# Letting the planner of a hybrid RWKV-7 / DeltaNet layer count TensorE's instructions, with ranks set anew

## The chip, the cores and the metric

One core of one Trainium2 chip runs the whole layer in one launch. The metric is device time in microseconds (us), lower is better. Three runs of the kernel before took 2218.86, 2225.49 and 2235.87 us; the median is 2225.49.

## What is computed

One diffusion-backbone layer in fp32: 256 latent tokens and 256 context tokens, width 2048. The reference, cut to its stages:

```python
h  = modulate(rmsnorm(x, norm1_w), sh1, sc1)       # sh, sc, gt from silu(c) @ w_ada
hc = modulate(rmsnorm(ctx, norm1_w), csh1, csc1)
rw, cv, z, ab, gt = split(h @ w_in)                # the same for hc
o_a = rwkv_readout(bidirectional RWKV-7 scan of 16 heads x 64)     # context state starts the latents
o_b = gdn_readout(bidirectional chunked DeltaNet of 8 heads x 128) # triangular solve per chunk of 64
y = (sigmoid(g_a) * (o_a @ p_a) + sigmoid(g_b) * (o_b @ p_b)) @ w_out
x = x + gt1 * y
x = x + gt2 * swiglu(modulate(rmsnorm(x, norm2_w), sh2, sc2), w_gate_up, w_down)
return rmsnorm(x, final_norm_w)
```

## The kernel before

**Stages.** A first stage (to about 136 us) makes the modulation and the low-rank columns. Then comes the *weave* (about 136 to 1290 us): the input projection, the RWKV mixer in 8 pairs of heads and the DeltaNet mixer in 8 heads, interleaved. Behind it stand the products with `p_a`, `p_b`, `w_out` and the feed-forward part. Every large product is done in three fp32r matmuls, high by high, high by low and low by high; the weights are split into `whi` (a cast on ScalarE) and `wlo` (a subtraction on VectorE) after their load into `wraw`.

**Main products.** In the weave the generator `products()` makes the projection: a product is 16 k-steps of three matmuls `mm<-hxh,whi`, `mm<-hxl,whi`, `mm<-hxh,wlo`, 512 columns wide where context is needed and 256 wide otherwise. They need only weights and the input, so they serve as fill for TensorE. The 40 gate columns (`GATES_A`, `GATES_B`) are spread over pairs and heads by hand.

**Chains.** For each pair or head other generators carry the chain: `prepare`, `grams` (lists of 32 small matmuls, 64x64, into `pa`), `inverse` (`invert()`: two lists of 64 matmuls `pi<-arena` and `pi<-arena,Tx` with 32x16 outputs, then two of 32 with 32x32, with VectorE work between them), `scan`, `values`, and for heads `head_grams`, `head_inverse`, `head_scan`, `features`, `decays`, `tokens`. `lowrank` makes the matmuls `s<-lin,wraw`. `ada_rest` accumulates further modulation columns.

**What sets the order.** All five engines run their instructions in the order in which the weave hands them out. `Weave.run` is a greedy planner at build time: each generator holds one operation or one list of TensorE operations; for each it estimates the earliest start (engine free, last result plus `HOP`), and the smallest (start, rank) goes next. A list is cut to `LAT['grp']` = 32 operations for TensorE at a time; costs come from `Lane`. Ranks (`RANK`, plus 10 per pair or head) break ties, the lowest first; main products have rank 900. Outside the weave a scheduler of the framework sets the order.

**Lines.** In the profile every operation that the weave emits has line L147, the `return op` call of `Lane`. L370 and L371 are the split of the weights behind the weave, L380 to L382 the matmuls of `gemm`.

**Instruction size.** An fp32r matmul or a transpose becomes two of TensorE's instructions (a weight load and a matmul), a plain fp32 matmul four (two passes of each). So the 64 small fp32 matmuls of one `pi` list are 256 instructions. TensorE's instructions, 48234 with its semaphore waits, are fetched from memory while the kernel runs, by a DMA queue of kind "instruction".

Of the kernel before, what the change touches and what calls it, by code (L numbers as in the profile page):

```python
# [12 lines left out]
F32R = mybir.dt.float32r  # L13
# [11 lines left out]
NPAIR = 8  # L25
NGH = 8
DECAY = 0.6065306597126334
GATES_A, GATES_B = (6, 2, 3, 3, 0, 1, 4, 3), (2, 2, 0, 1, 0, 2, 10, 1)

RANK = dict(cast=-94, lowrank=60, prepare=59, grams=34, inverse=-56, values=6, scan=-39, begin=196, head_scan=145, head_inverse=100, head_grams=123, decays=137, tokens=77, features=120, gate_out=137, lowrank_out=105, row_tile=486)  # L30
LAT = dict(dma=2.04, hop=0.255, own=0.092, grp=32, cg=4, turn=0.17)
LNEXP = "natural_log_exp_and_others"
SIGM = "sigmoid_and_others"
UNIT = 64 * 64 + 64
# [65 lines left out]
        return t.rearrange(f"p ({' '.join(ax)}) -> p {' '.join(ax)}", **dict(zip(ax, shape[1:])))  # L100


HOP = LAT['hop']


# [7 lines left out]
class Lane:  # L113
# [5 lines left out]
    def __getattr__(self, name):  # L119

        def op(out, *a, **k):
            if name == "preload_act_table_set":
                return Op(self, 1.3, lambda: self.engine.preload_act_table_set(out))
            if name == "dma_start":
                return Op(self, 0.6 if self.each > 0.0012 else 0.33, lambda: self.engine.dma_start(out, *a))
            n = int(np.prod(out.shape[1:]))
            kind = "full"
            if name == "transpose" and len(a) == 2:
                cost = 0.109
            elif name == "matmul":  # L130
                rows, m = a[0].shape[0], out.shape[0]
                if a[0].dtype == F32R:
                    cost, kind = 0.0035 + 0.000448 * n, "split"
                elif rows <= 64 and m <= 64:
                    cost, kind = (0.01 + 0.00037 * n if rows < 64 else 0.01 + 0.00075 * n), (rows, m)
                elif m <= 64:
                    cost, kind = 0.058 if m == 64 else 0.14, (rows, m)
                else:
                    cost = (0.0054 + 0.00167 * n) * (1.22 if rows == 96 else 1)
            else:  # L140
                psum = a and getattr(a[0], "tensor", None) is not None and "PSum" in type(a[0].tensor).__name__
                cost = (self.psum if psum else self.fixed) + self.each * n
                if name == "tensor_tensor_scan":
                    cost *= 1.9
                elif name == "scalar_tensor_tensor" and not psum:
                    cost *= 1.2
            return Op(self, cost, lambda: getattr(self.engine, name)(out, *a, **k), kind)  # L147
        return op
# [33 lines left out]
        return self.pool.tile([P, 512], F32, tag=self.tag, name=self.tag)  # L182


class Weave:


# [2 lines left out]

    def __init__(self):
        self.work, self.free, self.done, self.now, self.kind = [], {}, {}, 0.0, "split"

    def add(self, rank, gen, at=None):
        now = self.now
# [45 lines left out]
    def run(self):  # L241
        while self.work:
            for w in list(self.work):
                if w[5] is not None and not isinstance(w[5], (list, float)) and self.there(w):
                    self.step(w, self.take(w))
            best = None
            for w in self.work:
                if isinstance(w[5], float):
                    key = (w[3], w[0])
                    if best is None or key < best[0]:  # L250
                        best = (key, w, None)
                elif isinstance(w[5], list):
                    lane = w[5][0].lane
                    at = w[3] + (0.0 if w[4] is None else lane.own if w[4] is lane else HOP)
                    key = (max(self.free.get(lane, 0.0), at), w[0])
                    if best is None or key < best[0]:
                        best = (key, w, lane)
            if best is None:
                if any(w[5] is not None and not isinstance(w[5], (list, float)) and self.there(w) for w in self.work):
                    continue  # L260
                assert not self.work, [w[5] for w in self.work]
                return
            (start, _), w, lane = best
            if lane is None:
                w[5] = None
                assert w[3] < 1e5, [x[5] for x in self.work]
                self.step(w, None)
                continue
            ops, rest, w[4] = w[5], None, lane
            if lane is self.tensor:  # L270
                ops, rest = ops[:LAT['grp']], ops[LAT['grp']:]
                if ops[0].kind != self.kind:
                    start += LAT["turn"] if isinstance(ops[0].kind, tuple) or isinstance(self.kind, tuple) else 0.02
                self.kind = ops[-1].kind
            w[5] = rest or None
            got = [o.call() for o in ops]
            w[3] = self.free[lane] = start + sum(o.cost for o in ops)
            if rest:
                w[4] = None
            else:  # L280
                self.step(w, got[-1])


def emit(ctx: ExitStack, tc, A, out, dbg=None):
    nc = tc.nc
    V, S, G, Q = nc.vector, nc.scalar, nc.gpsimd, nc.sync
    E = nc.tensor
    global weave
    weave = Weave()
    dq = Loads(Q)  # L290
# [131 lines left out]
    with tc.tile_pool(name="p0", bufs=1) as p0, \  # L422
# [100 lines left out]
        for part in range(NE + 1):  # L523
            if part < NE:
                ps = pst(pmm, "mm")
            for c in range(2):
# [6 lines left out]
                if c == 0 and part < NE:  # L533
                    w = low_split(part)
# [212 lines left out]
    def lowrank():  # L747
# [17 lines left out]
        for p in range(NPAIR):  # L765
# [12 lines left out]
            for j in (0, 2, 1, 3):  # L778
                ps = yield psb
                yield e.matmul(ps, w[:96, 4 * (p % 2) + j], lin[:, j], start=True, stop=True)  # L780
                weave.add(RANK['lowrank_out'], lowrank_out(p, j, ps, out[j]))

    def prepare(p):
# [75 lines left out]
        if p + 1 < NPAIR:  # L859
            weave.add(10 * p + 10 + RANK['prepare'], prepare(p + 1))  # L860

# [220 lines left out]
    def products():  # L1082
# [24 lines left out]
        while todo or nxt:  # L1107
            if nxt is None:
# [4 lines left out]
                if nxt[0] == "g":  # L1113
                    nxt = "g", next(gate_next)
                weave.add(RANK['cast'], cast(source(*nxt), i))
            what, p = nxt
# [3 lines left out]
            for k in range(KT):  # L1120
                if k == 4:
                    nxt = choose()
                    if nxt is not None:
                        if nxt[0] == "g":
                            nxt = "g", next(gate_next)
                        weave.add(RANK['cast'], cast(source(*nxt), i + 1))
                if k % LAT['cg'] == 0:
# [7 lines left out]
            if what == "g":  # L1135
                weave.add(RANK['gate_out'], gate_out(rs, p, ps))
            else:
# [9 lines left out]
    first = {"laR": [P, 2, 4, 2, 64], "KB": [P, 2, 8, 64], "VX0": [P, 8, 2, 64], "VX1": [P, 8, 2, 64], "KBx": [P, 2, 8, 2, 64],  # L1147
             "ivx": [P, 16, 64], "Y": [P, 4, 64], "bon": [P, T], "y2": [P, T], "y3": [P, T]}

    class Shared:  # L1150


        def __init__(self):
            self.arena = Places(None, arena, *gplaces)
            self.inX = [None, None]
# [475 lines left out]
    for j in range(KT):  # L1631
# [13 lines left out]
        elif j % 3 == 2 and j < 12:  # L1645
            hi, lo = (W4[:, i, j // 3] for i in range(2))
            for c in range(2):
                k, raw = slice(8 * c, 8 * c + 8), coming.pop(0)
# [3 lines left out]
    r = rms_scale(x1p, [ssum, sq], T, "rs")  # L1652
# [6 lines left out]
    with tc.tile_pool(name="fp", bufs=1, reuse_waits="tile") as fp:  # L1659
# [19 lines left out]
        for j in range(NH):  # L1679
# [12 lines left out]
            if 2 <= j < 34:  # L1692

                for a in range(2):
                    c = (j - 2) // 2
                    i = 2 * (j % 2) + a
                    w = fp.tile([P, 512], F32, tag="aw", name="aw", bufs=3)
# [19 lines left out]
        r = rms_scale(x1p, [ssum, sq], T, "rs", keep=True)  # L1717
# [99 lines left out]
```

## Time and profile before

| | |
|---|---|
| median of 3 runs | 2225.49 us (2218.86 to 2235.87) |
| the profiled execution | 2228.24 us, span 2226.1 us |
| TensorE (PE) busy | 2117.7 us, 95% |
| VectorE (DVE) busy | 1571.3 us, 71% |
| ScalarE (ACT) busy | 1068.5 us, 48% |
| mean granted TensorE clock | 0.982 |

The span runs from the first to the last instruction; the execution's own time is 2.1 us more. Busy PE time is modelled from start times, so a row's duration overlaps the next row; start to start is the better measure of what a matmul costs. In the timeline, `[1.74 <-issue]` behind a row says that the engine was idle 1.74 us before it and waited for no semaphore that the profile shows. The granted clock of a stretch is a share of full speed.

### The profile page before, as it was taken

To read this page: it belongs to the slowest core of one execution; us is meant where nothing else is said; L and a number is where in the kernel's file an instruction comes from. 1 tells how busy PE (TensorE), PEld (TensorE's weight loads), DVE (VectorE), ACT (ScalarE), POOL (GpSimd) and SP (SyncE) were. 2 spreads that over 40 slices of the span, in tenths; PEclk is the share of its full clock that TensorE was granted. 3 is DMA by queue.
4 is the path that set the end of the run, shared out by engine and by line. 5 is a ranking of instruction groups with operands and counts; after the bars stand their busy time and mean duration, and the time that the engine had idled before them with its cause. 6 is when DMAs were issued, how large, how long until landed. Compare 5 with 4: busy or idle time off the path is not lost.

```text
span 2226.1 us, 56729 instructions
## 1 busy us (share of the span) xinstructions
PE 2117.7 (95%) x23996; PEld 1913.4 (86%) x23996; DVE 1571.3 (71%) x3197; ACT 1068.5 (48%) x1853; POOL 120.4 (5%) x203
## 2 busy tenths in 40 slices
PE   6998899899999999999999989999999999999998
PEld 3875678778888778878788889999999999999997
DVE  3456778787988778999998778855666665444454
ACT  3258745544454455445554455534444444444443
POOL 0000100100000011011110010100000000000000
PEclk9999899999999999999999999999999999999999
DMA  9966444444444445566567797937777776566665
GB/s 385 413 181 180 133 121 112 111 114 115 118 119 139 112 146 164 175 180 184 172 201 239 257 339 257 348 100 225 235 235 235 236 236 203 190 186 186 190 190 160
DMA packets 234494, 435.29 MB, mean 196 GB/s; under 512 B 115328, under 2 KB 129664, under 8 KB 229888
## 3 DMA queue, kind: packets, MB, share of 16 engines
q1 hardware_dynamic: 206304, 355.11, 50.8%
q0 software_dynamic: 14112, 51.39, 7.2%
q10 hardware_dynamic: 13824, 25.17, 3.4%
q8 instruction: 188, 3.08, 0.6%
q14 instruction: 66, 0.54, 0.1%
HBM read 405.76 MB, written 25.84 MB: 194 GB/s over the span
## 4 chain that ended last, share of the span: by engine, by line
issue 45%; PE 29%; DVE 12%; DMA 9%; ACT 3%; POOL 1%; SPq 1%; POOLq 0%; DVEq 0%; ACTq 0%
PE mm L147 14%; PE pa L147 5%; DVE arena L147 4%; DVE wlo L147 2%; PE s L147 2%; PE pi L147 2%; PE mm L382 1%; PE mm L381 1%; PE mm L380 1%; DMA aw<-ada_rest 1%; DMA aw<-ada_first 1%; DVE aw L147 1%; ACT arena L147 1%; PE mm L475 1%; DMA wr<-wgu 1%
## 5 line engine op out<-in xcount | busy, mean ns | idle before, releaser
L371 DVE TENSOR_TENSOR wlo<-wraw,whi 128x1024 fp32r<-128x1024 f32 x328 | 392.7, 1198 | 318.7 <-ACT whi L370 316.0
L370 ACT CAST whi<-wraw 128x1024 fp32r<-128x1024 f32 x328 | 336.9, 1028 | 463.3 <-PE mm L381 409.2
L147 PE MATMUL mm<-hxh,wlo 128*128 128x256 f32 (+1 forms) x1376 | 465.3, 338 | 10.0 <-DVE wlo L147 9.2
L147 PE MATMUL mm<-hxh,whi 128*128 128x256 f32 (+1 forms) x1376 | 463.8, 337 | 2.0 <-DVE arena L147 1.2
L147 PE MATMUL mm<-hxl,whi 128*128 128x256 f32 (+1 forms) x1376 | 461.1, 335 | 0.0
L382 PE MATMUL mm<-hfh,wlo 128*128 128x256 f32 x1344 | 375.1, 279 | 0.4 <-DVE wlo L371 0.4
L380 PE MATMUL mm<-hfh,whi 128*128 128x256 f32 x1344 | 375.0, 279 | 0.0
L381 PE MATMUL mm<-hfl,whi 128*128 128x256 f32 x1344 | 374.9, 279 | 0.0
L147 PEld LDWEIGHTS mm<-hxh,wlo 128*128 128x128 f32 x1376 | 263.1, 191 | 39.6 <-DVE wlo L147 14.4
L147 PEld LDWEIGHTS mm<-hxh,whi 128*128 128x128 f32 x1376 | 263.3, 191 | 25.6 <-issue 5.6
L147 PEld LDWEIGHTS mm<-hxl,whi 128*128 128x128 f32 x1376 | 263.4, 191 | 23.6 <-issue 3.9
L147 DVE TENSOR_TENSOR wlo<-wraw,whi 128x512 fp32r<-128x512 f32 x344 | 239.9, 698 | 34.9 <-ACT whi L147 33.5
L147 ACT CAST whi<-wraw 128x512 fp32r<-128x512 f32 x344 | 204.5, 616 | 110.6 <-PE mm L147 84.4
L382 PEld LDWEIGHTS mm<-hfh,wlo 128*128 128x128 f32 x1344 | 252.8, 188 | 0.7 <-DVE wlo L371 0.6
L380 PEld LDWEIGHTS mm<-hfh,whi 128*128 128x128 f32 x1344 | 252.9, 188 | 0.0
L381 PEld LDWEIGHTS mm<-hfl,whi 128*128 128x128 f32 x1344 | 252.8, 188 | 0.0
L147 DVE TENSOR_TENSOR arena<-arena 128x28 f32<-128x28 f32 (+12 forms) x538 | 139.0, 261 | 23.5 <-DMA arena<-scr 9.2
L380 PE MATMUL mm<-za,whi 128*128 128x256 f32 x512 | 142.9, 279 | 0.0
L382 PE MATMUL mm<-za,wlo 128*128 128x256 f32 x512 | 142.7, 279 | 0.0
L381 PE MATMUL mm<-za,whi 128*128 128x256 f32 x512 | 142.7, 279 | 0.0
L147 ACT ACTIVATE arena<-arena 128x512 f32<-128x512 f32 (+2 forms) x132 | 76.4, 593 | 76.4 <-DVE arena L147 59.5
L380 PEld LDWEIGHTS mm<-za,whi 128*128 128x128 f32 x512 | 96.3, 188 | 0.0
(332 smaller groups left out, 3943.6 us busy)
## 6 DMA issues: line engine op xcount, KB each, us to landing
wraw<-w SPq DMA_DIRECT2D x172, 512.0 KB, 4.0
wraw<-wgu SPq DMA_DIRECT2D x168, 512.0 KB, 4.6
aw<-ada_rest POOLq DMA_DIRECT2D x96, 512.0 KB, 5.2
aw<-ada_first SPq DMA_DIRECT2D x32, 1024.0 KB, 13.2
wraw<-wdn SPq DMA_DIRECT2D x64, 448.0 KB, 3.6
wraw<-wout SPq DMA_DIRECT2D x32, 512.0 KB, 6.9
aw<-ada_gt ACTq DMA_DIRECT2D x64, 256.0 KB, 4.8
wraw<-wdn SPq DMA_DIRECT2D x32, 512.0 KB, 3.7
```

What stands on the lines that cost most here:

```text
L147: return Op(self, cost, lambda: getattr(self.engine, name)(out, *a, **k), kind)
L370: S.copy(hi[:, c, :M], raw[:, c, :M])
L371: V.tensor_sub(lo[:, c, :M], raw[:, c, :M], hi[:, c, :M].bitcast(F32))
L380: E.matmul(ps, hi, Xh[:, k, :n], start=first and i == 0, stop=False)
L381: E.matmul(ps, hi, Xl[:, k, :n], start=False, stop=False)
L382: E.matmul(ps, lo, Xh[:, k, :n], start=False, stop=last and i == len(wt) - 1)
L475: E.matmul(ps[32 * g:32 * g + 32, 0:P], ckr[:, k].rearrange("p a b -> p (a b)"), aws[e, c][:, i, g], start=k == 0, stop=k == KT - 1)
```

## The change

The planner gets a count of TensorE's instructions. A wrapper `Words` around the engine counts two or four for each matmul or transpose emitted, from the start of the program. `Weave.late` walks through a list and asks at each block boundary (every 256 instructions, the first at 193) whether the block would be there: it was asked for 40 instructions before the previous boundary, or when the block before arrived, and comes 4.2 us later. What is missing is added to the list's estimated start, so another generator, most often `products()`, may go first. Operations keep their costs; transposes become a kind of their own ("turn"), which adds the small cost of 0.02 us at a change of kind to the plan. At the same time `RANK`, the hop and the gates per pair and head are set to other numbers; the sums of the gates stay 22 and 18. With the wrapper every matmul has line L198.

```diff
-GATES_A, GATES_B = (6, 2, 3, 3, 0, 1, 4, 3), (2, 2, 0, 1, 0, 2, 10, 1)
+GATES_A, GATES_B = (6, 3, 2, 3, 0, 1, 4, 3), (3, 2, 0, 1, 1, 1, 9, 1)
-RANK = dict(cast=-94, lowrank=60, ... inverse=-56, values=6, scan=-39, ... head_grams=123, decays=137, tokens=77, ...
+RANK = dict(cast=-98, lowrank=164, ... inverse=-70, values=-6, scan=-95, ... head_grams=132, decays=132, tokens=73, ...
+BLOCK = dict(size=256, first=193, ahead=40, time=4.2, base=8, waits=1.0072)
+class Words:
+        def op(out, a, *r, **k):
+            self.n += (2 if name == "transpose" or a.dtype == F32R else 4) * BLOCK["waits"]
+            return getattr(self.engine, name)(out, a, *r, **k)
...
+    def late(self, ops, start):
+        n, t, b, here, asked, late = self.tensor.engine.n, start, self.block, self.here, self.asked, 0.0
+        if b is None:
+            b = int(n - BLOCK["first"]) // BLOCK["size"] + 1
+        for o in ops:
+            edge = BLOCK["first"] + BLOCK["size"] * b
+            if asked is None and n >= edge - BLOCK["ahead"]:
+                asked = max(t, here)
+            if n >= edge:
+                if t < here:
+                    late += here - t
+                    t = here
+                b, here, asked = b + 1, (t if asked is None else asked) + BLOCK["time"], None
+            n += self.words(o) * BLOCK["waits"]
+            t += o.cost
+        return late, (b, here, asked)
...
-                    at = w[3] + (0.0 if w[4] is None else lane.own if w[4] is lane else HOP)
-                    key = (max(self.free.get(lane, 0.0), at), w[0])
+                    at = max(self.free.get(lane, 0.0), w[3] + (0.0 if w[4] is None else lane.own if w[4] is lane else HOP))
+                    if lane is self.tensor and (best is None or at <= best[0][0]):
+                        at += self.late(w[5][:LAT["grp"]], at)[0]
+                    key = (at, w[0])
```

What it moves is seen in TensorE's rows. **The first pair's inverse.** Before, the list of 64 in `inverse(0)` is followed at once by the `grams` list of the second pair (rows of two, which go on below):

```order
L147 MATMUL s<-lin,wraw 128x512
L147 MATMUL mm<-hxh,wlo 128x512
L147 MATMUL pi<-arena 32x16 x64
L147 MATMUL pa<-kh,arena 64x64 x2
L147 MATMUL pa<-arena,kh 64x64 x2
```

Now that `grams` list stands ahead, a low-rank matmul lies between the two, and main products follow the list:

```order
L198 MATMUL pa<-kh,arena 64x64 x2
L198 MATMUL pa<-arena,kh 64x64 x2
L198 MATMUL s<-lin,wraw 128x512
L198 MATMUL pi<-arena 32x16 x64
L198 MATMUL s<-lin,wraw 128x512
L198 MATMUL mm<-hxl,whi 128x512
```

The rows show that the 256 instructions of `pi` no longer have another small list right behind them; the `grams` list itself now follows main and low-rank matmuls.

**The second pair's inverse.** Before, its two lists of 64 stood with one list of 16 (the readout of the first pair's scan) between them:

```order
L147 MATMUL mm<-hxh,wlo 128x512
L147 MATMUL pi<-arena 32x16 x64
L147 MATMUL s<-laR,VX 64x64 x16
L147 MATMUL pi<-arena,Tx 32x16 x64
L147 MATMUL pa<-sgd,g_3568 128x256
L147 MATMUL pa<-C,arena 128x128 x2
```

Now that readout stands ahead of both, and wide work lies between the two lists:

```order
L198 MATMUL s<-laR,VX 64x64 x16
L198 MATMUL pi<-arena 32x16 x64
L198 MATMUL pa<-sgd,g_3573 128x256
L198 MATMUL pa<-C,arena 128x128 x2
L198 MATMUL mm<-hxl,whi 128x512
L198 MATMUL mm<-hxh,wlo 128x512
L198 MATMUL mm<-hxh,whi 128x512
L198 MATMUL pa<-Y,C 128x256
...
L198 MATMUL pa<-C,arena 128x128 x2
L198 MATMUL pi<-arena,Tx 32x16 x64
L198 MATMUL pa<-y_3639,C 128x256
```

Seven main matmuls, two 256-wide fp32 matmuls and four transposes have come between the lists of 64.

**The end of the weave.** Before, the last main products stood behind the last head's inverse, among the first matmuls of its `head_scan` (`s<-TF,keg`):

```order
L147 MATMUL s<-TF_10841,keg 128x128 x3
L147 MATMUL pa<-C,arow 128x128 x2
L147 MATMUL mm<-hxh,whi 128x256
L147 MATMUL mm<-hxl,whi 128x256
...
L147 MATMUL s<-TF_10841,keg 128x128 x3
L147 MATMUL s<-inX,TF_10841 128x128 x2
L380 MATMUL mm<-oah,whi 128x256 x2
```

Now they end inside that inverse, and the products with `p_a` (`mm<-oah,whi` and its kin) fill from there on:

```order
L198 MATMUL pi<-inX,qo 32x32 x16
L198 MATMUL mm<-hxh,wlo 128x256
L198 MATMUL mm<-oah,whi 128x256 x2
L198 MATMUL pi<-qo,inX 32x32 x16
L198 MATMUL mm<-oal,whi 128x256
```

The last head's readout (`s<-arena,C`) stood behind 122 of the 384 matmuls with `p_a`, and now stands behind 242.

More of the change, by code (lines that the diff above doesn't have):

```diff
@@ L27 @@
 DECAY = 0.6065306597126334
-GATES_A, GATES_B = (6, 2, 3, 3, 0, 1, 4, 3), (2, 2, 0, 1, 0, 2, 10, 1)
-RANK = dict(cast=-94, lowrank=60, prepare=59, grams=34, inverse=-56, values=6, scan=-39, begin=196, head_scan=145, head_inverse=100, head_grams=123, decays=137, tokens=77, features=120, gate_out=137, lowrank_out=105, row_tile=486)
-LAT = dict(dma=2.04, hop=0.255, own=0.092, grp=32, cg=4, turn=0.17)
+GATES_A, GATES_B = (6, 3, 2, 3, 0, 1, 4, 3), (3, 2, 0, 1, 1, 1, 9, 1)
+RANK = dict(cast=-98, lowrank=164, prepare=59, grams=34, inverse=-70, values=-6, scan=-95, begin=196, head_scan=145, head_inverse=100, head_grams=132, decays=132, tokens=73, features=120, gate_out=137, lowrank_out=105, row_tile=496)
+LAT = dict(dma=2.04, hop=0.2729, own=0.092, grp=32, cg=4, turn=0.17)
 LNEXP = "natural_log_exp_and_others"
@@ L128, in op @@
             if name == "transpose" and len(a) == 2:
-                cost = 0.109
+                cost, kind = 0.109, "turn"
             elif name == "matmul":
@@ L182, in tile, with __init__, __getattr__ @@
         return self.pool.tile([P, 512], F32, tag=self.tag, name=self.tag)
+class Words:
+    def __init__(self, engine):
+        self.engine, self.n = engine, BLOCK["base"]
+    def __getattr__(self, name):
+        if name not in ("matmul", "transpose"):
+            return getattr(self.engine, name)
+        def op(out, a, *r, **k):
+            self.n += (2 if name == "transpose" or a.dtype == F32R else 4) * BLOCK["waits"]
+            return getattr(self.engine, name)(out, a, *r, **k)
+        return op
 class Weave:
@@ L192, in __init__, with words @@
         self.work, self.free, self.done, self.now, self.kind = [], {}, {}, 0.0, "split"
+        self.block, self.here, self.asked = None, 0.0, None
+    def words(self, op):
+        return 2 if op.kind in ("split", "turn") else 4
+    def late(self, ops, start):
[14 more added lines that the diff above has]
+        return late, (b, here, asked)
     def add(self, rank, gen, at=None):
@@ L274, in run @@
                 self.kind = ops[-1].kind
+                self.block, self.here, self.asked = self.late(ops, start)[1]
             w[5] = rest or None
@@ L286, in emit @@
     V, S, G, Q = nc.vector, nc.scalar, nc.gpsimd, nc.sync
-    E = nc.tensor
+    E = Words(nc.tensor)
     global weave
```

## Prediction

> **What bounds the kernel now.** I read the page first, then TensorE's waits, then the timeline around the longest stops, then the granted clock.
>
> ```profile
> span 2226.1 us, 56729 instructions
> PE 2117.7 (95%) x23996; PEld 1913.4 (86%) x23996; DVE 1571.3 (71%) x3197; ACT 1068.5 (48%) x1853; POOL 120.4 (5%) x203
> q8 instruction: 188, 3.08, 0.6%
> ```
>
> TensorE is the bound, so a gain must come from its idle time or from a slow clock. The third row (queue, packets, MB, share) matters here: 188 packets bring 3.08 MB, 16 KB each; over TensorE's 48234 instructions that is one packet for 256. TensorE's waits, in total, times, longest:
>
> ```profile
> PE pi L147 <- issue: 11.8, 8, 2.2
> PE mm L147 <- DVE wlo L147: 9.2, 13, 2.0
> PE s L147 <- DVE Vn L147: 6.2, 7, 2.1
> PE pa L147 <- issue: 4.1, 3, 1.8
> ```
>
> The first and last row are 11 stops of **15.9 us** in which TensorE waited for nothing that the profile shows. The middle rows are ordinary waits for VectorE. Where the 11 lie, the timeline shows:
>
> ```profile
> 242.32 0.23 PE L147 MATMUL pa<-arena,kh 64*64 64x64 f32 x2
> 244.28 0.37 PE L147 MATMUL pa<-kh,arena 64*64 64x64 f32 x2 [1.74 <-issue]
> ...
> 317.36 0.31 PE L147 MATMUL pi<-arena 32*32 32x16 f32 x14 [0.48 <-issue]
> 321.63 0.57 PE L147 MATMUL pi<-arena,Tx 32*32 32x16 f32 x46 [2.08 <-issue]
> 416.80 1.88 PE L147 MATMUL pi<-arena,Tx 32*32 32x16 f32 x123 [1.22 <-issue]
> 420.92 0.81 PE L147 MATMUL pa<-laR,arena 64*64 64x64 f32 x20 [1.82 <-issue]
> ```
>
> A stop falls in the middle of a list that needs no new data. Counted along TensorE's rows, all 11 stand at instruction 193 plus a multiple of 256, within two. Consecutive stops end 321.63 - 317.36 = 4.27 and 420.92 - 416.80 = 4.12 us apart. I read this as: a block of 256 instructions comes no faster than one in some 4.2 us. How fast a list eats a block:
>
> ```profile
> L147 PE MATMUL pi<-arena,Tx 32*32 32x16 f32 x1024 | 12.6, 188 | 10.0 <-issue 9.4 <-DVE arena L147 0.6
> L147 PE MATMUL pa<-KB,X 64*64 64x64 f32 x1024 | 19.1, 221 | 0.0
> ```
>
> A pass of the first kind costs 12.6/1024 = 0.012 us, so 64 matmuls (128 passes, one whole block) take 1.6 us; the second kind's 0.019 us makes 2.4 us. Two such lists in a row must stop.
>
> [...]
>
> A second cost follows the stops. These stretches, found by the clock's steps, begin with or soon after a stop and run at half clock (columns: length, busy PE, PEld, DVE, ACT, POOL, granted clock, DMA):
>
> ```profile
> 244.32:254.56 10.24, 10.24 (x180) 6.89 (x180) 7.51 (x16) 5.01 (x11) 0.00 (x0) 0.50 0.48 157
> 322.83:326.24 3.41, 3.41 (x10) 2.74 (x11) 2.06 (x7) 2.96 (x10) 0.00 (x0) 0.50 0.06 17
> 414.99:425.23 10.24, 6.89 (x175) 6.45 (x176) 6.82 (x16) 1.03 (x4) 0.00 (x0) 0.50 0.41 111
> 486.67:490.08 3.41, 3.41 (x52) 3.27 (x44) 3.13 (x10) 1.63 (x5) 0.00 (x0) 0.50 0.22 59
> 548.11:551.52 3.41, 3.41 (x18) 3.04 (x18) 2.65 (x7) 1.30 (x5) 0.00 (x0) 0.50 0.02 5
> 626.61:630.03 3.42, 3.42 (x19) 3.42 (x18) 3.35 (x7) 1.58 (x6) 0.00 (x0) 0.50 0.03 8
> 766.56:773.39 6.83, 5.82 (x50) 4.73 (x51) 4.13 (x9) 3.84 (x11) 1.01 (x3) 0.50 0.24 80
> sum 40.96, PE 36.61 PEld 30.53 DVE 29.65 ACT 17.33 POOL 1.01; mean PE 5.23 PEld 4.36 DVE 4.24 ACT 2.48 POOL 0.14
> ```
>
> What half clock does to a main matmul (256 wide), inside the sixth stretch and behind it:
>
> ```profile
> 628.93 0.41 PE L147 MATMUL mm<-hxh,whi 128*128 128x256 f32 x1
> 629.14 0.41 PE L147 MATMUL mm<-hxl,whi 128*128 128x256 f32 x1
> ...
> 632.03 0.28 PE L147 MATMUL mm<-hxh,whi 128*128 128x256 f32 x1
> 632.14 0.28 PE L147 MATMUL mm<-hxl,whi 128*128 128x256 f32 x1
> ```
>
> Start to start it is 0.21 us against 0.11. So the 36.61 us of busy time would be half as long at full clock: 18.3 us lost at most. The small lists do not slow down as much (123 passes took 1.88 us from 416.80 on), so I take **16.5 us**.
>
> [...]
>
> **The change part by part.** No computation is added or removed: 18298 matmuls stand in both programs, the gates add up to 40 in both, and the counting runs at build time. So every term is one of order.
>
> *Stops.* I counted both orders in groups of 296 instructions (a block and the 40 by which, in the kernel's table, the request runs ahead), each matmul at its mean start-to-start time in this trace (as 0.012 and 0.019 us above; 0.11 to 0.12 for a main matmul 256 wide, about twice that for 512). Before, 15 groups take under 4.2 us and lack 20.1 us together, the worst 2.4; the trace has 15.9. After, 7 groups lack 1.9 us together, the worst 0.5. The count misses single stops by up to 1.7 us either way, and 13 more groups lie within 0.8 us above 4.2, so I leave 3.5 us of stops. Gain 15.9 - 3.5 = 12.4 us; bounds 0 and 15.9.
>
> *Clock.* Of the 16.5 us I leave 1.5 for the stops that stay: gain 15; bounds 0 (small lists alone might keep the clock down) and 18.3.
>
> *Order of chains.* A list put back delays its chain. The second pair's `pi<-arena,Tx` waits for seven main matmuls 512 wide, about 7 x 0.23 = 1.6 us, where it stood still 2.08 us before: no net delay. The rank of `lowrank`, 60 to 164, puts the low-rank rows behind the pairs' lists where both could start; their last row stands beside the first inverse in both orders, so later pairs see little of it. What is bought early is missing late. The tail has cover, as the timeline shows (the last head's readout, its end on VectorE, and the next use of `oah`):
>
> ```profile
> 1290.17 0.70 PE L147 MATMUL s<-arena,C 128*128 128x256 f32 x2 [0.34 <-ACT arena L147]
> 1295.59 0.48 DVE L147 SCALAR_TENSOR_TENSOR arena<-arena,PR 128x256 f32<-128x256 f32 x1
> 1323.80 2.19 ACT L385 CAST oah<-arena 128x512 fp32r<-128x512 f32 x4
> ```
>
> The readout ends 5.9 us after its first row, and the next stage begins 27.7 us later, when the products with `p_a` are through. Now 142 of those matmuls remain behind the readout instead of 262: 142 x 0.117 = 16.6 us, still over 5.9. I cost it at nothing; if the last chain slips by more than 16.6 - 5.9 = 10.7 us, each further microsecond costs one. Between the bounds (all DVE waits of the two rows above gone, -15.4; a slip past the cover, up to +35) I take 0, the nearest row being the cover.
>
> *Sum.* The profiled execution took 2228.24 us, 2.1 over its span and 2.7 over the median of 2225.49. 2228.2 - 12.4 - 15 = 2200.8, **2201 us**. A change of 1% (22 us, about what a measurement of this kernel can tell) is 2203, so the forecast lies just beyond.
>
> **The rivals.**
>
> *The stops turn into waits.* Stops go, but lists that went back make VectorE's or ScalarE's part of the chain end last. For it speaks the second row here, a stretch in which VectorE is 94% busy (149.93 of 160; the first row is the readout of the head before the last):
>
> ```profile
> 1234.03 0.70 PE L147 MATMUL s<-arena,C 128*128 128x256 f32 x2
> ...
> 960.00:1120.00 160.00, 153.60 (x1622) 129.60 (x1621) 149.93 (x400) 84.84 (x168) 19.62 (x30) 1.00 0.60 179
> ```
>
> Against it: the 11 stops lie before 770 us, and their fill costs the pairs no more than the stop did. If half of 27.4 us comes back as waits: 2214.
>
> *The new ranks also close VectorE waits.* The rows `wlo` and `Vn` hold 15.4 us; all of that beyond my sum gives 2185. For it: 20 waits with main products as possible fill. Against: nothing in the change shortens a VectorE step.
>
> *The stops are not the fetch's.* Then a new order leaves as many: 2222 to 2232. [...] The 11 places at 193 + 256k speak against it.
>
> *Slower: the last chain outruns its cover.* The last two readouts start 1290.17 - 1234.03 = 56 us apart. If VectorE, at 94%, stretches each of the eight heads by 7 us, the last readout comes 56 us later than in my sum; 10.7 are covered, 45 are lost: 2201 + 45 = 2246. It is slower than before from a slip of 10.7 + 27.4 = 38 us on. Against it: at the times counted above, the last head's inverse stands only 8 us of TensorE's work later than before.
>
> **How the numbers follow.** Forecast (2190 to 2212): 0.53, two thirds of it under 2203. Waits instead of stops (2207 to 2222): 0.22. VectorE waits closed too (2178 to 2190): 0.14. No effect: 0.06. Slower: 0.05, about half of it over 2248. Under 2203 lies 0.35 + 0.14 plus a trifle, 0.50; slower by over 1% 0.03; the rest 0.47. The range 2184 to 2222 leaves out the end of the third case, the fourth's upper half and the fifth.
>
> **What would show it.** Right: the two "issue" rows of TensorE fall from 15.9 to under 5 us, the seven half-clock stretches fall to two or three, `pi<-arena,Tx` loses its 9.4 us of issue, and the weave ends about 27 us sooner. Wrong on order: the rows of `wlo`, `Vn` and `pi <- DVE` grow by what the issue rows lose. Wrong on the clock: the stops are gone and stretches at 0.50 remain between 240 and 780 us. The stages from `p_b` on should take what they took.

## The result, and the profile after

| | before | after |
|---|---|---|
| median of 7 runs | 2223.42 us | 2204.0 us (2202.31 to 2207.0) |
| ratio, 95% interval | | 0.9912 (0.9889 to 0.9935) |
| the profiled execution | 2228.24 us | 2203.45 us |
| mean granted clock | 0.982 | 0.988 |

The change makes the kernel 0.9% faster, 19.4 us between the medians; 2201 was forecast. The page's rows (span; busy time of the engines; the queue that brings TensorE's instructions: packets, MB, share):

```profile
span 2201.7 us, 56730 instructions
PE 2107.9 (96%) x23996; PEld 1906.1 (87%) x23996; DVE 1576.0 (72%) x3197; ACT 1068.0 (49%) x1852; POOL 121.7 (6%) x203
q8 instruction: 188, 3.08, 0.6%
```

TensorE's 23996 passes and their 188 packets are the same; of the other engines only ScalarE has one instruction fewer. TensorE's waits after (engine, output, line, what it waited for; us in total, times, longest):

```profile
PE mm L198 <- DVE wlo L148: 9.3, 11, 3.1
PE s L198 <- DVE VX L148: 6.5, 11, 2.3
PE s L198 <- DVE Vn L148: 2.4, 5, 1.0
PE pi L198 <- issue: 2.1, 4, 0.9
PE pa L198 <- issue: 0.5, 1, 0.5
```

The two "issue" rows fell from 15.9 us in 11 stops to 2.6 us in 5. `wlo` kept its 9 us (9.2 before), `Vn` lost 3.8 (6.2 before), and `VX` has 6.5 (2.9 before). The inverse of the second pair, where a stop of 2.08 us stood at 321.63, shows the edit at work in TensorE's timeline (start, length, instruction, count; in brackets idle time before it):

```profile
316.29 1.26 PE L198 MATMUL pi<-arena 32*32 32x16 f32 x128
317.48 0.70 PE L198 MATMUL pa<-sgd,g 64*128 64x256 f32 x2
...
320.75 1.26 PE L198 MATMUL pi<-arena,Tx 32*32 32x16 f32 x128
```

Both lists of 64 run through, 1.26 us each, and wide work stands between them, from 317.48 to 320.75 us. What is left at half clock in the weave, in the table of windows (length; busy PE, PEld, DVE, ACT, POOL; granted clock; DMA share and GB/s):

```profile
245.49:252.32 6.83, 6.68 (x94) 4.38 (x98) 5.19 (x11) 3.51 (x7) 0.00 (x0) 0.50 0.53 153
344.47:347.88 3.41, 3.41 (x17) 3.41 (x17) 3.34 (x8) 1.51 (x6) 0.00 (x0) 0.50 0.31 105
597.06:600.47 3.41, 3.41 (x77) 3.15 (x75) 0.51 (x2) 0.00 (x0) 0.00 (x0) 0.50 0.50 159
791.62:798.45 6.83, 4.82 (x70) 3.72 (x71) 4.33 (x8) 4.90 (x6) 0.00 (x0) 0.50 0.37 85
...
sum 37.54, PE 33.45 PEld 29.30 DVE 26.35 ACT 17.86 POOL 1.23; mean PE 4.18 PEld 3.66 DVE 3.29 ACT 2.23 POOL 0.15
```

The sum is of all eight stretches between 136 us and the first matmul with `w_out`, 37.5 us; before, there were twelve, 58.0 us. Up to 800 us there were nine, 47.8 us: the prediction's seven (40.96) and two ahead of them, at 206.8 and 234.1. Now it is 20.5 us in the four shown.

**Where the time went.** I cut both traces at the start of the first matmul with `w_out`, found in the view of the tile `mh`. Rows of the kernel before, then of the changed one:

```profile
L380 PE MATMUL mm<-mh,whi x22: 274/280/283, 1372.3 to 1379.7; 128*128 128x256 f32 x22
```

```profile
L198 PE MATMUL mm<-mh,whi x78: 274/280/384, 1351.5 to 1379.8; 128*128 128x256 f32 x78
```

It starts 1372.3 - 1351.5 = 20.8 us sooner; the rest of the span is 24.4 - 20.8 = 3.6 us shorter too. From 136 us to that place I added up TensorE's idle gaps of over 0.1 us, and the extra time of each matmul that started at half clock against the mean of its kind at full clock. Idle time went from 70.7 to 55.8 us (-14.9, of which 13.3 are the "issue" rows), half clock cost 15.2 instead of 25.2 (-10.0), and what is left over, 4.1 us the other way, lies in the other matmuls.

### The profile page after: what moved, and what is told of

Its sections match the earlier page's. It is cut to its first block, busy times and chain, and to the rows that moved or that the text cites. A ratio compares the mean times of both kernels' runs of the same rounds, so it can differ in the third digit from the quotient of the medians.

```text
span 2201.7 us, 56730 instructions
## 1 busy us (share of the span) xinstructions
PE 2107.9 (96%) x23996; PEld 1906.1 (87%) x23996; DVE 1576.0 (72%) x3197; ACT 1068.0 (49%) x1852; POOL 121.7 (6%) x203
## 3 DMA queue, kind: packets, MB, share of 16 engines
q1 hardware_dynamic: 206304, 355.11, 51.4%
## 4 chain that ended last, share of the span: by engine, by line
issue 41%; PE 11%; DVE 6%; DMA 3%; ACT 1%; POOL 1%; SPq 0%; POOLq 0%; DVEq 0%; ACTq 0%
PE mm L198 8%; DVE arena L148 2%; DMA aw<-ada_rest 2%; PE s L198 1%; DVE wlo L148 1%; DVE aw L148 1%; PE pa L198 1%; DMA wraw<-pa 1%; DVE inX L148 1%; PE pi L198 0%; DMA arena<-grow 0%; DVE wlo L413 0%; DMA inX<-tscr 0%; DVE LT L148 0%; ACT arena L148 0%
## 5 line engine op out<-in xcount | busy, mean ns | idle before, releaser
L198 PE MATMUL mm<-hxh,wlo 128*128 128x256 f32 (+1 forms) x1408 | 474.8, 337 | 10.0 <-DVE wlo L148 9.3
L198 PE MATMUL mm<-hxh,whi 128*128 128x256 f32 (+1 forms) x1408 | 476.0, 338 | 5.7 <-ACT whi L148 3.2
L198 PE MATMUL mm<-hxl,whi 128*128 128x256 f32 (+1 forms) x1408 | 472.0, 335 | 0.0
L198 PE MATMUL mm<-hfh,wlo 128*128 128x256 f32 x1344 | 375.5, 279 | 0.4 <-DVE wlo L413 0.4
L198 PE MATMUL mm<-hfh,whi 128*128 128x256 f32 x1344 | 375.2, 279 | 0.0
L198 PE MATMUL mm<-hfl,whi 128*128 128x256 f32 x1344 | 375.2, 279 | 0.0
L198 PEld LDWEIGHTS mm<-hxh,wlo 128*128 128x128 f32 x1408 | 267.3, 190 | 39.1 <-DVE wlo L148 14.3
L198 PEld LDWEIGHTS mm<-hxh,whi 128*128 128x128 f32 x1408 | 267.4, 190 | 32.3 <-issue 6.8
L198 PEld LDWEIGHTS mm<-hxl,whi 128*128 128x128 f32 x1408 | 267.6, 190 | 24.6 <-issue 4.4
L198 PEld LDWEIGHTS mm<-hfh,wlo 128*128 128x128 f32 x1344 | 252.6, 188 | 0.7 <-DVE wlo L413 0.6
L198 PEld LDWEIGHTS mm<-hfl,whi 128*128 128x128 f32 x1344 | 252.6, 188 | 0.0
L198 PEld LDWEIGHTS mm<-hfh,whi 128*128 128x128 f32 x1344 | 252.6, 188 | 0.0
L198 PE MATMUL mm<-za,whi 128*128 128x256 f32 x1024 | 180.2, 279 | 0.0
L198 PEld LDWEIGHTS mm<-za,whi 128*128 128x128 f32 x1024 | 156.1, 188 | 0.1
L148 DVE TENSOR_TENSOR arena<-arena 128x28 f32<-128x28 f32 (+13 forms) x538 | 138.9, 260 | 19.3 <-DMA arena<-scr 8.5
L198 PE MATMUL mm<-za,wlo 128*128 128x256 f32 x512 | 142.9, 279 | 0.0
L148 ACT ACTIVATE arena<-arena 128x512 f32<-128x512 f32 (+3 forms) x132 | 76.3, 592 | 72.1 <-DVE arena L148 49.2
L198 PEld LDWEIGHTS mm<-za,wlo 128*128 128x128 f32 x512 | 96.2, 188 | 0.0
```

What stands on the lines that cost most here:

```text
L198: return getattr(self.engine, name)(out, a, *r, **k)
```

## The experiments

The theory: TensorE stops where a block of 256 instructions is late, the counting planner puts wide work in front of such places, and half clock follows the stops. Rivals: the new ranks alone make the better order; any new order would; half clock has another cause.

**1. Each part alone.** The count with the old numbers, the new numbers without the count, and a new order from the hop alone in the kernel before:

```diff
 count_alone (the changed kernel)
-GATES_A, GATES_B = (6, 3, 2, 3, 0, 1, 4, 3), (3, 2, 0, 1, 1, 1, 9, 1)
+GATES_A, GATES_B = (6, 2, 3, 3, 0, 1, 4, 3), (2, 2, 0, 1, 0, 2, 10, 1)
 and RANK and hop as before
 ranks_alone (the changed kernel)
-BLOCK = dict(size=256, first=193, ahead=40, time=4.2, base=8, waits=1.0072)
+BLOCK = dict(size=256, first=193, ahead=40, time=0.0, base=8, waits=1.0072)
 hop_only (the kernel before)
-LAT = dict(dma=2.04, hop=0.255, own=0.092, grp=32, cg=4, turn=0.17)
+LAT = dict(dma=2.04, hop=0.2729, own=0.092, grp=32, cg=4, turn=0.17)
```

> Only the planner's count is added; ranks, gates and hop stay as before. Counted in groups of 296 instructions at the mean times of the trace of before, 9 groups lack 7.0 us (before 15 groups and 20.1, after 7 and 1.9). Theory (stops of the fetch and the half clock behind them): TensorE's issue rows fall to about 5 us, time about 2210. Rival (the new ranks made the gain): issue rows may fall, the time stays at 2220 to 2226 because the waits for VectorE grow.

> Ranks, gates and hop of after, but a block is taken to arrive at once (time 0), so nothing is put back. 14 groups lack 16.7 us. Theory: issue rows of about 13 us, time 2217 to 2222. Rival (the ranks made the gain): about 2205.

> The kernel before with one number of the plan moved (hop 0.255 to 0.2729), as a measure of what any new order does. 20 groups lack 21.6 us. Theory: issue rows of 14 to 18 us and a time of 2218 to 2230. Rival (any new order shifts the time by tens of us, so the result is luck): a time outside that.

| kernel | median us | ratio to before, 95% | "issue" | half clock in the weave |
|---|---|---|---|---|
| count_alone | 2230.85 | 1.0001 (0.9982 to 1.002) | 7.7 | 64.9 |
| ranks_alone | 2233.63 | 1.0018 (0.9998 to 1.0037) | 9.9 | 58.0 |
| hop_only | 2229.82 | 1.0001 (0.9982 to 1.0021) | 17.4 | 75.1 |

TensorE's "issue" rows of the first two:

```profile
PE pi L198 <- issue: 7.0, 3, 3.5
PE mm L198 <- issue: 0.7, 1, 0.7
```

```profile
PE pi L198 <- issue: 7.7, 5, 2.7
PE pa L198 <- issue: 2.2, 1, 2.2
```

Neither part gains anything, and both expectations of a gain (about 2210, and 2217 to 2222) missed: fewer stops alone did not shorten the launch. The count alone halves the stops, but its plan loses the 8 us elsewhere: the stretches at half clock grew by 6.9 us, and TensorE's waits for ScalarE from 19.2 to 23.2. The ranks alone cut the stops by 6 and add 5.8 us of waits for VectorE (40.9 to 46.7; these sums are of the whole launch without the waits for `sq` in the first stage). So these ranks pay nothing without the count, nor does the count with the old ranks, and one other order, the hop's, gives nothing, as expected. Whether ranks searched for without the count could do as well was not tried.

**2. The same order, the block boundaries moved.** The changed kernel with 34 matmuls 32x32 that the planner doesn't count, 136 instructions, at the program's start where TensorE waits for data. All later rows stand in the same order, but every boundary falls 136 instructions earlier in it.

```diff
         ps = pst(pa, "pa")
+        for _ in range(34):
+            nc.tensor.matmul(ps[0:32, 0:16], ident[0:32, 0:32], ident[0:32, 0:16], start=True, stop=True)
```

> The program of after with 34 tiny fp32 matmuls (136 instructions) in the first stage, where TensorE waits about 10 us for squares anyway; the planner does not count them, so the order of all else is the same and only the block boundaries lie elsewhere. 10 groups lack 10.9 us instead of 1.9. Theory: issue rows rise from 2.6 to about 8 to 9 us, more half-clock stretches, time 2212 to 2218. Rival (order and waits made the gain, not the boundaries): 2204 to 2205.

> The order of after with the block boundaries 136 instructions elsewhere, now beside after on one chip. In the first run its issue rows were 5.4 us against 2.6. Theory: 3 to 8 us slower than after on the same chip. Rival (boundaries don't matter): the same within 2 us.

> The changed kernel on the same chip as the others: ratio 0.989 to 0.993 to before, issue rows of 2 to 4 us.

It took 2212.74 us, ratio to before 0.9922 (0.9898 to 0.9946); on the chip of the changed kernel's repeat, 2209.11, 0.9931 (0.9908 to 0.9955), against that kernel's 2202.05, 0.989 (0.9866 to 0.9913). The "issue" rows in the second pair of runs, shifted and then unshifted:

```profile
PE pi L198 <- issue: 3.1, 4, 1.2
PE pa L198 <- issue: 2.3, 2, 1.4
```

```profile
PE pi L198 <- issue: 1.7, 3, 0.8
PE pa L198 <- issue: 0.5, 1, 0.5
```

With the order held, moving the boundaries alone brings 3.2 us of stops and 10.3 us more half clock (34.1 to 44.4), which costs at most half of that, 5 us (in the changed kernel main matmuls 256 wide start 0.21 us apart from 597.1 us on, at half clock, and 0.12 just ahead): together up to 8.4, measured 7.1 between medians. The 10.3 is rough: the two traces of the unshifted kernel differ by a stretch (37.5 and 34.1 us), and the first shifted one had 41.0. Both shifted traces have 5.4 us of stops, where the first expectation had 8 to 9. Counted along TensorE's rows, every stop of over 0.15 us in the ten traces of before, after and experiments 1 to 3, 57 in all, stands at 193 plus a multiple of 256, within one, and in the shifted runs that is 136 instructions earlier in the order. This shows that the stops belong to the block boundaries, and that a part of the gain is a fit to where they fall. About two thirds of the gain stay; that wide work between the lists helps wherever the boundary falls is how I read it, and was not tried at other places.

**3. The lists made shorter.** In both lists of 64 of each inverse, two 32x32 matmuls became one of 64x64, so a list is 128 instructions instead of 256; the planner still saw 64, so the order stays in the kernel before and nearly so in the changed one. (These kernels compute other inverses: each block takes in its neighbour.)

```diff
-yield [e.matmul(pv[r, 0, u], Lt(h, u)[b:b + 32, b:b + 32], T0[r, u, ...], start=True, stop=True) for h, u, b, r in fours]
+yield merged([...], [lambda ...: E.matmul(pv[r, 0, u], Lt(h, u), T0[r, u, ...], start=True, stop=True)
+                     for h, u, b, r in fours if b == 0])
```

> The order of before on every engine, unchanged; in the two lists of 64 of each inverse two 32x32 matmuls are replaced by one of 64x64 on the same rows (the inverses then come out as other numbers), so a list is 128 instructions and not 256. 2 groups lack 1.2 us instead of 15 and 20.1. The merged lists themselves save little: 2048 passes at 0.012 us against 1024 at about 0.019, some 5 us. Theory (stops and the half clock behind them cost about 25 us): TensorE's issue rows fall from 15.9 to about 1 us, fewer half-clock stretches, time 20 to 30 us below before (ratio 0.987 to 0.991). Rival (order made the gain of the change, the stops are filled by waits that would come anyway): 5 to 8 us below before.

> The same replacement in after, the planner counting as before so that the order stays (the inverses come out as other numbers): a measure of what the merged lists save by themselves where hardly a stop is left. Theory: 4 to 10 us below after. Rival: if merged lists alone save much more, the result of the other kernel says little on stops.

In the order of before: 2207.38 us, 0.9916 (0.9892 to 0.994). In the changed order: 2219.26, 0.9961 (0.9943 to 0.9979), so 17.2 us slower than the changed kernel beside it, where 4 to 10 us faster was expected. I had expected the merged lists to be cheaper by some 5 us; the groups of the merged kernel (busy us, mean ns; idle) show them dearer:

```profile
L651 PE MATMUL pi<-arena,Tx 64*64 64x16 f32 x512 | 18.7, 218 | 0.5 <-DVE arena L147 0.4
L644 PE MATMUL pi<-arena 64*64 64x16 f32 x512 | 17.7, 209 | 2.8 <-DVE arena L147 2.4 <-DMA arena<-tscr 0.4
```

36.4 us against the 12.6 + 11.4 before, though there are half as many. And yet the kernel before gained 19.7 us by it: its stops fell from 15.9 to 0.2 us, and all idle time in the weave from 70.7 to 45.9. So idle time fell by more than the stops' own 15.9 us; that the rest, waits for other engines, hung on the stops is not shown, for the lists themselves last 12.4 us longer. In the changed order, where one stop of 1.1 us is left, the longer lists come with 54.6 us at half clock instead of 34.1. Half clock costs at most half of these 20.5 us more; with the longer lists that is enough for the loss.

The kernel of before with merged lists also tells on the clock. Three of its stretches at half clock:

```profile
408.19:415.02 6.83, 6.83 (x90) 6.71 (x87) 5.90 (x14) 1.38 (x5) 0.00 (x0) 0.50 0.55 149
534.48:548.13 13.65, 13.65 (x123) 12.99 (x120) 9.51 (x22) 5.28 (x14) 2.45 (x4) 0.50 0.12 40
616.40:619.81 3.41, 3.41 (x18) 3.41 (x18) 3.34 (x7) 1.47 (x5) 0.00 (x0) 0.50 0.42 153
```

There is one stop of 0.2 us in the whole program, and still 54.6 us of the weave run at half clock, at a cost of 25.1 us, as much as before. So half clock came here without the stops, and in part without waits. The window of 3.41 us just ahead of the third stretch, and the sum of the windows ahead of these three and of a fourth stretch (756.35 us):

```profile
612.99:616.40 3.41, 3.31 (x103) 3.00 (x95) 3.37 (x9) 0.00 (x0) 0.00 (x0) 1.00 0.24 44
...
sum 13.64, PE 12.89 PEld 10.72 DVE 10.05 ACT 5.14 POOL 1.38; mean PE 3.22 PEld 2.68 DVE 2.51 ACT 1.29 POOL 0.35
```

TensorE was busy for 12.89 of 13.64 us there, more than half of it with small lists. These four stretches are 27.3 of the 54.6 us; ahead of the other seven TensorE waited 1.4 to 3.2 us for other engines.

**4. The lists by themselves.** Lists of matmuls of the identity at the program's start, where nothing else runs, once all in one place of the array and once in its two or four places in turn (the loop shown):

```diff
         ps = pst(pa, "pa")
+        for m, n, r, c in ((1, 64, 128, 128), (1, 512, 32, 16), (1, 64, 128, 128), (1, 512, 64, 64), (1, 64, 128, 128),
+                           (8, 64, 32, 16), (1, 64, 128, 128), (16, 64, 32, 16), (1, 64, 128, 128), (1, 128, 32, 128), (1, 64, 128, 128)):
+            for i in range(n if m == 1 else 8 * (n + m)):
+                if m > 1 and i % (n + m) >= n:
+                    nc.tensor.matmul(ps[:, 0:P], ident, ident, start=True, stop=True)
+                else:
+                    p = slice(i % (P // r) * r, i % (P // r) * r + r)
+                    nc.tensor.matmul(ps[p, 0:c], ident[p, p], ident[p, 0:c], start=True, stop=True)
```

> The changed kernel with six kinds of lists put by themselves into the first stage, where nothing else runs on TensorE (plain fp32 matmuls of the identity into a tile that is overwritten; four instructions each): 64 matmuls 128x128 with 128 columns before, between and behind the others; then 64 of 64x64 with 128 columns, 64 of 32x32 with 128 columns, 512 of 32x32 with 16 columns, 512 of 64x64 with 64 columns, 512 of 128x128 with 16 columns. The launch should take 130 to 200 us more than 2202; only the rows of the lists are of interest. Theory of the blocks (one of 256 instructions per 4.2 us, the stop in the middle of a list): 512 matmuls of 32x32 are 2048 instructions, 8 blocks, so their list takes 8 x 4.2 = 34 us with stops of some 2.6 us, one per block, not the 12.6 us that its passes take; 512 of 64x64 also take 34 us, not 19.5. If blocks are fetched well ahead, they take 12.6 and 19.5 us and stop nowhere. Theory of the clock A (work of the array decides, columns times the share of the 128x128 array that is used): the lists of 32x32 and 64x64 run at half clock from the second window of 3.41 us on, the 32x32 list with 128 columns too, though TensorE has no idle time there and no block is late (64 matmuls of some 0.2 us are 256 instructions in 13 us); full clock comes back within a window or two of each 128x128 list. Theory B (the stops, idle time, decide): the two lists with 128 columns keep clock 1.00; only lists with stops lose it.

> The lists by themselves again, but matmul i stands in place i modulo 4 (32x32) or i modulo 2 (64x64) of the array, as in the kernel's own lists, where consecutive ones overlap. Between lists of 64 matmuls 128x128 with 128 columns (14.5 us each at full clock): 512 of 32x32 with 16 columns; 512 of 64x64 with 64 columns; eight times 64 of 32x32 with 8 of 128x128 behind each; eight times the same with 16; 128 of 32x32 with 128 columns. Only these rows are of interest. Theory of the blocks (256 instructions come at most once in 4.2 us, asked for 296 instructions ahead): the first list is 8 blocks and takes 8 x 4.2 = 34 us with stops of some 2.6 us, not the 12.6 that 1024 passes take in the kernel; the second 34, not 19.5; the third has 288 instructions a turn, 8 x 288/256 x 4.2 = 38 us with stops of some 1.2 us in each turn, not 8 x 3.4 = 27; the fourth has 320 a turn in 5.2 us, one block in 4.2, and stops nowhere by more than 0.3 us. If blocks are fetched far ahead: 12.6, 19.5, 27 and 42 us without a stop. Clock: by the array's work (columns times share of the array) the first list, with or without stops, runs at half clock, the second only if its stops bring its share under about 0.2 (0.35 without, 0.2 with them), the third is near the border, the fourth (over half the time 128x128) keeps 1.00, and the last (two passes at a quarter share between four places) keeps 1.00 although it is all 32x32.

In one place (2636.38 us in all, 434 over the changed kernel's 2202, where 130 to 200 was expected), the question of the blocks wasn't put: 1024 passes of 32x32 took 51.4 us, 0.050 each and not 0.012, so 256 instructions took 6.4 us and no list stopped. In four places the list of 512 shows it (timeline, then windows with DMA share):

```profile
28.33 1.90 PE L504 MATMUL pa<-C 32*32 32x16 f32 x128 [4.69 <-issue]
34.52 1.90 PE L504 MATMUL pa<-C 32*32 32x16 f32 x128 [4.29 <-issue]
37.98 1.90 PE L504 MATMUL pa<-C 32*32 32x16 f32 x128 [1.55 <-issue]
41.98 1.90 PE L504 MATMUL pa<-C 32*32 32x16 f32 x128 [2.10 <-issue]
45.98 1.90 PE L504 MATMUL pa<-C 32*32 32x16 f32 x128 [2.10 <-issue]
```

```profile
28.33:34.52 6.19, 1.90 (x128) 1.80 (x128) 0.00 (x0) 0.00 (x0) 0.00 (x0) 0.50 0.94 380
37.98:53.99 16.01, 7.60 (x513) 7.18 (x513) 0.00 (x0) 0.00 (x0) 0.00 (x0) 0.50 0.02 4
```

The list stops every 128 passes, 256 instructions, and waits for nothing else: it takes 33.0 us, where 34 was expected with late blocks and 12.6 without. With the DMA engines 2% busy, the last ones come each 4.00 us; while the first loads keep the DMA engines 94% busy, one took 6.19. The second list, 512 of 64x64 in two places, took 30.0 us without a stop, where 34 or 19.5 was expected: its passes last 0.029 us, so it uses up 256 instructions in 3.75 us, at a granted clock of 1.00, and no block was late for that.

The mixed lists correct the size. With 8 wide matmuls behind each 64, the eight turns took 33.3 us, not 38; the stops were 0.24 to 0.51 us (1.2 expected) but for one of 2.56, and most of their ends lie some 3.45 us apart. With 16, where nothing over 0.3 was expected, two turns of eight stopped:

```profile
177.37 1.24 PE L504 MATMUL pa<-C 32*32 32x16 f32 x127
179.99 0.17 PE L504 MATMUL pa<-C 32*32 32x16 f32 x1 [1.38 <-issue]
```

There the boundary falls on the list's last pass, so the one before stands just ahead of the list: 1.24 + 1.38 = 2.6 us passed between them. If the block had been asked for 40 instructions before the previous boundary (ten wide matmuls here, 2.3 us), it would have taken some 4.9 us to come; in the turns with 8, blocks came 3.45 apart. The 40 is a number of the kernel's table: no run shows it, and these two turns agree with it only if their block was slower than the others.

The clock, from windows of the lists in one place (64x64 and 32x32 with 128 columns, 64x64 with 64, 128x128 with 16; granted clock third from the end):

```profile
22.32:36.43 14.11, 14.11 (x129) 13.94 (x128) 0.00 (x0) 0.00 (x0) 0.00 (x0) 1.00 0.84 341
55.12:74.39 19.27, 19.27 (x92) 15.25 (x89) 0.00 (x0) 0.00 (x0) 0.00 (x0) 0.50 0.00 1
159.20:219.06 59.86, 59.86 (x1025) 59.80 (x1024) 0.00 (x0) 0.00 (x0) 0.00 (x0) 1.00 0.01 2
236.03:449.40 213.38, 213.38 (x1002) 213.38 (x1002) 0.00 (x0) 0.00 (x0) 0.00 (x0) 0.50 0.00 1
```

and of the 32x32 list with 128 columns in four places:

```profile
222.94:230.06 7.12, 7.12 (x258) 6.92 (x257) 0.00 (x0) 0.00 (x0) 0.00 (x0) 1.00 0.02 5
```

TensorE is busy all the time in all five, and no block is late. The same 32x32 matmuls run at half clock in one place (1/16 of the array at work, shares being of a 128x128 tile, the largest in these rows) and at full clock in four (1/16 at 0.028 us a pass, where a pass of 128 columns by itself took 0.11: about a quarter). A quarter of the array (64x64) ran at 1.00, and the whole array with 16 columns, an eighth of a pass of 128, at 0.50. So the theory that the array's work decides fits these lists (0.50 at a sixteenth and an eighth, 1.00 at a quarter), and the theory of stops alone falls. Two expectations missed: both 64x64 lists kept the clock in one place, and the turns with 16 lost it around their two stops (0.92 on average from 163 to 208 us).

## Why the prediction was right or wrong

- **The bound** was TensorE, rightly: the whole gain is its idle time and its clock.
- **Stops.** The forecast left 3.5 us and gained 12.4; 2.6 are left, 13.3 gained. The cause was right (the moved boundaries show it; the list of 512 in four places shows the period, 4.00 us). Groups of 296 instructions and 4.2 us per block were good enough for this sum, but some 3 us off for three other orders (7.7 for about 5 in `count_alone`, 9.9 for 13 in `ranks_alone`, 5.4 for 8 to 9 in the shifted runs). As a model of single stops they are not good: the mixed lists had stops of 0.24 to 0.51 us where 1.2 was expected, and 1.38 where 0.3 was. Of most 3.45 us from stop to stop in the turns with 8, TensorE stood still for only 0.24 to 0.51. The list of 64x64 in two places, which used up 256 instructions in 3.75 us, had no stop.
- **Clock: the step that failed.** "A second cost follows the stops", 16.5 us of which 15 were to go. The forecast kept half clock for the stops that stay and for nothing else (1.5 us of the 16.5), and it left out five of the twelve stretches of before, 17.0 us, that follow no stop. 10.0 went in the whole weave, and four stretches stay before 800 us where two or three were forecast. Three of them (245, 344 and 597 us) lie between 240 and 780 us, the prediction's own sign of being wrong on the clock.

  What the runs show in its place: in the traces of before, after and the merged kernel each stretch of the weave at half clock follows 3.41 us in which TensorE stood still for a part of the time or ran mostly small lists. Some have a stop there: before, six of the twelve stretches have one in the window ahead, and in the second shifted run the stretches at 397.2 and 475.7 us follow stops of 1.4 and 1.2 us. Some have a wait for another engine: the other six of before (206.8, 234.1, 415.0, 950.9, 1162.5 and 1299.0 us) have waits of 1.3 to 3.1 us ahead and no stop; the third in the prediction's table, 414.99, is one of them and begins 0.6 us ahead of its stop. And some have small lists with hardly a wait: ahead of four stretches of the merged kernel TensorE was busy for 12.89 of 13.64 us; so the lower bound's reason, that small lists alone might keep the clock down, came true there. In the changed kernel, though, all eight stretches that are left follow waits for VectorE, ScalarE or a DMA, and none a stop. Rows ahead of the first two, then the windows ahead of these two and the sum of all eight windows:

```profile
243.63 0.69 PE L198 MATMUL pi<-arena 32*32 32x16 f32 x60 [2.39 <-DMA arena<-tscr]
245.64 1.05 PE L198 MATMUL pi<-arena 32*32 32x16 f32 x64 [1.32 <-DVE arena L148]
344.26 0.42 PE L198 MATMUL mm<-hxh,wlo 128*128 128x256 f32 x1 [1.92 <-DVE wlo L148]
```

```profile
242.08:245.49 3.41, 0.69 (x60) 0.59 (x60) 1.81 (x3) 1.57 (x3) 0.00 (x0) 1.00 0.87 308
341.06:344.47 3.41, 1.49 (x12) 1.29 (x12) 3.38 (x4) 3.19 (x7) 3.02 (x5) 1.00 0.74 231
...
sum 27.28, PE 11.97 PEld 9.99 DVE 22.79 ACT 13.57 POOL 5.54; mean PE 1.50 PEld 1.25 DVE 2.85 ACT 1.70 POOL 0.69
```

  TensorE was busy for 12.0 of these 27.3 us. So half clock came behind the waits that this order leaves or makes, too, and the forecast's clock term left them out. How the 10.0 us gained divide between stops and wide work among the lists is not shown.

- **Order of chains**, costed at nothing: over the whole launch, without the waits for `sq` in the first stage, TensorE's waits for VectorE went from 40.9 to 39.2 us, for ScalarE from 19.2 to 16.8, for DMA from 9.1 to 10.2, and matmuls outside half clock lost 4.1 in the weave. Near nothing, as summed, but not because nothing moved: `Vn` lost 3.8 and `VX` gained 3.6, and `wlo` has one wait of 3.1 us, with a stretch at half clock (846.23 us) 1.9 us behind it.
- **The tail's cover** held. The last two matmuls of the last readout start at 1287.84 (1290.17 before), and the products with `p_a` are through 15.3 us later, where 16.6 was forecast (rows of TensorE, VectorE and ScalarE):

```profile
1287.84 0.59 PE L198 MATMUL s<-arena,C 128*128 128x256 f32 x2
1295.83 0.48 DVE L148 SCALAR_TENSOR_TENSOR arena<-arena,PR 128x256 f32<-128x256 f32 x1
1303.17 2.78 ACT L427 CAST oah<-arena 128x512 fp32r<-128x512 f32 x4 [1.25 <-PE mm L198]
```

  The readout needed 8.5 us of them, not 5.9, so 6.9 of cover are left.
- **The sum.** Forecast 27.4 us; between the profiled executions 24.8, between the medians 19.4. The first contains 3.6 us behind the weave that the edit doesn't touch: before, 6.8 us from 1469.7 ran at half clock, after not. "The stages from `p_b` on should take what they took" is right but for this. That leaves 20.8 in the weave, which is nearer to what the medians show: the clock's term was 5 us too large, and other matmuls took back 4. The chance of faster by over 1% and of the case below it were close to even, and the result is just below. That 2201 lies only 3 us from the measured 2204, with a gain 8 us too large, is in part luck: the sum started at the profiled 2228.24, and the seven runs of before have a median of 2223.42.
- **The rivals.** Stops that turn into waits: not in this order, but that is what became of the count alone. VectorE waits closed too: the rows `wlo` and `Vn` fell from 15.4 to 11.7 us, but others grew, and all waits for VectorE fell by 1.7. Stops that aren't the fetch's: no, by the moved boundaries. Slower by the last chain: no, its readout came 2.3 us sooner.

## What to carry to other kernels

Where "issue" stands in the rows of TensorE's waits, count its instructions: here all 57 stood at 193 plus a multiple of 256, and wide work of the same program put between small lists took most of them away (15.9 to 2.6 us) without a change to the lists. For each stretch at half clock, look at the 3.41 us ahead of it: here a stop, a wait for another engine or small lists stood there. The turns with 8 wide matmuls ran at 0.50 for 6.83 us around their one long stop, of 2.56 us, and at full clock elsewhere (16 wide passes took 3.78 us there, 2.05 in the other turns); 32x32 lists with 128 columns ran at 1.00 in four places of the array, at 0.50 in one. A planner's new cost term and the ranks that were set under it are one edit; here each alone was worth nothing (1.0001 and 1.0018 of before).

## What the runs showed of the hardware that was not expected

- Half clock came without idle time: the 32x32 list with 128 columns in one place ran at 0.50 for 19.27 us, with TensorE busy throughout. In the weave its stretches last 3.41, 6.83, 10.24 or, in the merged kernel, 13.65 us. They followed windows of 3.41 us with 1.3 to 3.1 us of waits in them (six stretches of before), and small lists with hardly any (12.89 of 13.64 us busy in the merged kernel). In ten traces of these kernels I set each window's columns times its share of the array against a window full of main matmuls, plain fp32 passes counted once: of 71 windows at full clock with less than about 22%, 61 were followed by half clock; between that and 44%, 40 of 198; above 55%, none of 2807 (in before and after alone, 136 to 1300 us: 11 of 16, 9 of 40, none of 537). The count orders the windows but doesn't settle them: by it the 64x64 lists in one place stand at 12 to 13%, and they ran at 1.00.
- Consecutive small matmuls started closer together in different places of the array than in one (with other output rows too; the runs change both at once): 1024 passes of 32x32 with 16 columns took 51.4 us in one place (0.050 each, most of them at half clock), against 0.015 at half clock in four places (1.90 us for 128) and 0.012 in the kernel's own lists. The merged 64x64 lists were dearer for all their fewer instructions (36.4 us against 24.0).
- A block of 256 instructions came each 4.00 us with the DMA engines 2% busy, at half clock, and in 6.19 us when they were 94% busy; in the turns with 8 wide matmuls most came 3.45 us apart, at full clock (2.05 us for 16 wide passes, and 3.78 at half).
- At half clock a pass of 128x128 with 16 columns took 0.211 us (216.1 us for 1024), nearly as long as one with 128 columns at that clock (0.232 in the lists in four places, 16 from 140.79 to 144.50 us).
